# Second attention of a two-layer decoder: values stationary, weights of both heads moving, division ahead of the transposes

## The chip, the cores and the metric

The kernel runs on one core of one Trainium2 chip. The metric is the device time of one execution in microseconds (us); lower is better. The median of 3 runs before the change is 977.81 us (977.59 to 978.05).

## The reference

A decoder trunk of two layers works on one sequence of 256 tokens with 1024 features, in fp32. Each layer is a half-step SwiGLU network, an attention, and a second half-step network, each behind an RMS norm and a modulation computed from a vector `c`. Layer 1 has a differential attention. Layer 2 has the attention that the change touches, a "forgetting" attention with 16 heads of 64 features:

```python
def forgetting_attention(h, w_q, w_o, k, v, F):
    ...
        decay = jnp.transpose(Fqb, (0, 2, 1))[..., None] - F_k[:, :, None, :]
        logits = jnp.einsum('bqhd,bkhd->bhqk', qb, k).astype(jnp.float32) * scale + decay
        logits = jnp.where(causal, logits, -jnp.inf)
        p = jax.nn.softmax(logits, axis=-1)
        return jnp.einsum('bhqk,bkhd->bqhd', p.astype(v.dtype), v)
    ...
    return o.reshape(b, s, B_WIDTH) @ w_o
```

Keys, values and the cumulated forget gates `F` were computed before from the residual stream. With 256 tokens there are two query tiles of 128: tile 0 attends to key block 0, tile 1 to key blocks 0 and 1.

## The kernel before, in words

Activations lie with the features on the partitions and the 256 tokens along the free dimension. All big products run as three fp32r matmuls, since every weight piece is split into a high part `wh` (copied by ScalarE, "ACT") and a low part `wl` (subtracted by VectorE, "DVE"), 1024 columns at a time. The pieces of all layers form one stream (`stream`, L230 to L261) and pass through rings of 6 raw, 6 high and 5 low buffers, so the split runs up to five pieces ahead of their use.

The order of work on each of TensorE ("PE"), ACT and DVE is the order in which the program issues it. The class `InOrder` (L54 to L100) keeps a rough clock for each of these engines at build time. The functions `bg`, `fill_act` and `fill_dve` (L351 to L385) use it to put the splits (`cp_part`, `sub_part`) between other instructions. GpSimd ("POOL") is issued directly; the planner does not know how long its work takes.

`attention_b` (from L1212) handles the 16 heads as 8 pairs `c`. For a pair it needs these steps:

- `load_g`, `decay` (POOL): a DMA that spreads a gate row over the partitions, issued from POOL, and four additions that make `d`, a tile of 384 columns for each head. Its columns are three blocks of 128: query tile 0 with key block 0, then query tile 1 with key blocks 0 and 1.
- `masked` (DVE): the causal mask is added to the two diagonal blocks of `d`, once for each head.
- `scores` (PE): four fp32 matmuls of queries and keys into the first 384 columns of the two banks `sb`, one for each head, with 64 partitions of contraction each.
- `exps`: four times a DVE pass that adds scores and `d` and finds the row extremes, and an ACT exponential with its row sums (`smb`).
- `weights_t` (PE), `weights_out`: six transposes of 128x128 into the banks `wa` and `wb`, copied out by ACT (512 columns, `wta`) and DVE (256 columns, `wtb`).
- `values` (PE): for each head three fp32 matmuls with a transposed weight block as the stationary operand and 64 value columns moving, into the second half of bank `wb`. The result has tokens on the partitions.
- `divide` (DVE): the reciprocal of the row sums and one multiplication of the result (`onb`).
- `out_t` (PE), `out_split`: two transposes into the last 128 columns of the two `sb` banks, so that features come onto the partitions; ACT writes the high part `obh` and DVE the low part `obl`, two instructions each.

These steps are spread over groups: group `t` does the scores and exponentials of pair `t`, the transposes of pair `t-1`, the values and division of pair `t-2`, and the output transposes of pair `t-3`. With 8 pairs there are 11 groups. Before each group stand fills, other PE work given out in small steps (`fills`, L1351): the two last query projections (`lq`) and six of the eight rows of the output projection (`pw`). The numbers of steps are the list in the loop at L1362. `masked(t+1)` and `decay(t+2)` end each group. `OutProj.finish` (L814) then does the last two rows of the output projection, whose inputs are the outputs of pairs 6 and 7, and eight fill steps that were left over.

Of the kernel before, what the change touches and what calls it, by code (L numbers as in the profile page):

```python
# [103 lines left out]
def trunk(ctx, tc, a, out):  # L104
    nc = tc.nc
    InOrder.ready = {}
    pe = InOrder(tc, nc.tensor, 0.0, 1 / 2350)
    act = InOrder(tc, nc.scalar, 0.13, 1 / 1200)
    dve = InOrder(tc, nc.vector, 0.08, 1 / 960)
# [5 lines left out]
    kp = ctx.enter_context(tc.tile_pool(name="kp", bufs=2))  # L115
# [5 lines left out]
    def sbank(name):  # L121
        return pp.tile([P, 512], F32, tag="s", name=name, bufs=2)
# [4 lines left out]
    def bbank(name):  # L127
        return pp.tile([P, 512], F32, tag="tb", name=name)

    mm = pe.matmul  # L130
# [1005 lines left out]
    op, rest = attention_a()  # L1136
# [75 lines left out]
    def attention_b():  # L1212
        ohs = [cp_.tile([P, 512], F32R, tag=f"hidh{j}", name=f"obh{j}") for j in range(4)]
        ols = [cp_.tile([P, 512], F32R, tag=f"hidl{4 + j}", name=f"obl{j}") for j in range(4)]
        o = [(ohs[c // 2][:, (c % 2) * 256:(c % 2) * 256 + 256],
              ols[c // 2][:, (c % 2) * 256:(c % 2) * 256 + 256]) for c in range(NC)]
        q = [cp_.tile([P, 512], F32, tag=f"hidl{j}", name=f"q{j}") for j in range(4)]
        gs, ds, sms = {}, {}, {}

        DT = [f"hidh{4 + j}" for j in range(4)] + ["hidl8", "hidl9"]  # L1220

        def load_g(c):
            g = cp_.tile([P, 512], F32, tag=("hidh10", "hidl10")[c % 2], name=f"fkb{c}")
            nc.gpsimd.dma_start(g, bass.AP(fdram.tensor, fdram.offset + 2 * c * S, [[0, P], [1, 2 * S]]))
            gs[c] = g

        def decay(c):

            for m in range(2):
                hd = 2 * c + m  # L1230
                d = cp_.tile([P, 384], F32, tag=DT[hd % 6], name=f"d{hd}")
                for qt, (c0, w) in enumerate(QT):
                    nc.gpsimd.tensor_scalar(d[:, c0:c0 + w], gs[c][:, m * S:m * S + w],
                                            Fq[:, qt * BH + hd:qt * BH + hd + 1], None, op0=ALU.add)
# [12 lines left out]
        for c in range(2):  # L1247
            load_g(c)
        for c in range(2):
            decay(c)  # L1250
        op = OutProj(o)
        st = {}
        mode[0] = "fill"
        NP = BH // 2

        def scores(c, sb):

            cb = (c % 2) * 256
            for qt, (c0, w) in enumerate(QT):
                for m in range(2):  # L1260
                    rows = slice(m * HD, m * HD + HD)
                    mm(sb[m][:, c0:c0 + w], q[c // 2][rows, cb + qt * P:cb + qt * P + P],
                       kT[c // 2][rows, cb:cb + w], start=True, stop=True)

        def exps(c, sb):
            nm = kp.tile([P, 4], F32, tag="nm", name=f"nmb{c}")
            sm = kp.tile([P, 4], F32, tag="smb", name=f"smb{c}", bufs=3)
            for m in range(2):
                d = ds[2 * c + m]
                for qt, (c0, w) in enumerate(QT):  # L1270
                    cc = 2 * qt + m
                    dve.tensor_tensor_reduce(
                        d[:, c0:c0 + w], sb[m][:, c0:c0 + w], d[:, c0:c0 + w], -0.125, BIG,
                        ALU.add, ALU.min, accum_out=nm[:, cc:cc + 1])
                    act.activation(d[:, c0:c0 + w], d[:, c0:c0 + w], AF.Exp,
                                   bias=nm[:, cc:cc + 1], scale=-1.0, accum_out=sm[:, cc:cc + 1])
            sms[c] = sm

        def weights_t(c, ta, tb):
            for j in range(6):  # L1280
                d, b = ds[2 * c + j // 3], j % 3
                pe.transpose(ta[:, j * P:j * P + P] if j < 4 else tb[:, (j - 4) * P:(j - 3) * P],
                             d[:, b * P:b * P + P], ident)

        def weights_out(c, ta, tb):
            w0 = cp_.tile([P, 512], F32, tag="hidh8", name=f"wta{c}")
            w1 = cp_.tile([P, 256], F32, tag="hidh9", name=f"wtb{c}")
            act.copy(w0, ta)
            dve.tensor_copy(w1, tb[:, :256])
            st[c] = [w0[:, j * P:j * P + P] for j in range(4)] + [w1[:, j * P:j * P + P] for j in range(2)]  # L1290

        def values(c, po):

            for m in range(2):
                hd = 2 * c + m
                wt = st[c][3 * m:3 * m + 3]
                vs = slice((hd % 8) * HD, (hd % 8) * HD + HD)
                v0, v1 = vb[0][hd // 8][:, vs], vb[1][hd // 8][:, vs]
                mm(po[:, m * HD:m * HD + HD], wt[0], v0, start=True, stop=True)
                mm(po[:, P + m * HD:P + m * HD + HD], wt[1], v0, start=True, stop=False)  # L1300
                mm(po[:, P + m * HD:P + m * HD + HD], wt[2], v1, start=False, stop=True)

        def divide(c, po):
            rs = kp.tile([P, 4], F32, tag="rs", name=f"rsb{c}")
            dve.reciprocal(rs, sms[c])
            on = kp.tile([P, 256], F32, tag="w512b", name=f"onb{c}")
            dve.tensor_tensor(on.rearrange("p (g d) -> p g d", g=4), po.rearrange("p (g d) -> p g d", g=4),
                              rs.rearrange("p (g o) -> p g o", o=1).to_broadcast([P, 4, HD]), op=ALU.mult)
            st[c] = on

        def out_t(c, pz):
            for qt in range(2):
                pe.transpose(pz[qt], st[c][:, qt * P:qt * P + P], ident)

        def out_split(c, pz):
            oh, ol = o[c]
            for qt in range(2):
                act.copy(oh[:, qt * P:qt * P + P], pz[qt])
            for qt in range(2):
                qs = slice(qt * P, qt * P + P)  # L1320
                dve.tensor_tensor(ol[:, qs], pz[qt], oh[:, qs].bitcast(F32), op=ALU.subtract)

        def group(t):

            cs, cw, cv, co = (c if 0 <= c < NP else None for c in (t, t - 1, t - 2, t - 3))
            sb = [sbank(f"sb{t}_{m}") for m in range(2)] if cs is not None or co is not None else None
            ta = abank(f"wa{t}") if cw is not None else None
            tb = bbank(f"wb{t}") if cw is not None or cv is not None else None
            if co is not None:
                pz = [sb[m][:, 384:] for m in range(2)]  # L1330
                out_t(co, pz)
            if cs is not None:
                scores(cs, sb)
            if cv is not None:
                values(cv, tb[:, 256:])
            if cw is not None:
                weights_t(cw, ta, tb)
            if co is not None:
                out_split(co, pz)
            if cs is not None:  # L1340
                exps(cs, sb)
            if cv is not None:
                divide(cv, tb[:, 256:])
            if cw is not None:
                weights_out(cw, ta, tb)
            if t + 1 < NP:
                masked(t + 1)
            if t + 2 < NP:
                decay(t + 2)

        def fills():  # L1351
            for j in (2, 3):
                for _ in late_pair("wq", q[j], r, f"lq{j}"):
                    yield
                    yield
            for _ in range(6):
                for _ in op.steps():
                    yield

        masked(0)  # L1360
        fill = fills()
        for t, n in enumerate((3, 9, 7, 7, 7, 7, 7, 7, 7, 6, 5)):  # L1362
            for _ in range(n):
                next(fill)
            group(t)
        return op, fill
# [135 lines left out]
```

## Time and profile before

| what | value |
|---|---|
| median of 3 runs | 977.81 us |
| the profiled execution, its own time | 978.77 us |
| its span, first to last instruction | 976.9 us |
| PE busy | 965.2 us (99%) |
| DVE busy | 815.0 us (83%) |
| ACT busy | 551.1 us (56%) |
| POOL busy | 82.0 us (8%) |
| granted TensorE clock | 0.998 |
| the second attention in the span | from about 717 to 789 us |

The profile is that of one execution. A group row gives the line, the engine, the operation, the tiles written and read (out<-in), the shapes and the count, then the busy time, the mean of one in ns, and the idle time of that engine just before, with what ended it. Nearly all rows have line L99, the place in `InOrder` where every instruction is issued, so tiles tell them apart. An fp32 matmul appears as two instructions, a transpose and an fp32r matmul as one. A row of a timeline gives start, length, engine, tiles and count; neighbouring instructions of one kind are merged in it, under the shape of the first. A row with engine shares gives a stretch of time and, for each engine in turn (PE, weight loads, DVE, ACT, POOL), how long it was busy in it. The ends of matmuls are modelled; starts are measured.

### The profile page before, as it was taken

The numbers are of one execution on the slowest core, as the hardware profiler recorded it, in microseconds if no ns is written. First come the engines' busy times: TensorE is split into PE (matmuls) and PEld (weight loads), VectorE is DVE, ScalarE is ACT, GpSimd is POOL, SyncE is SP. The second block draws the span as 40 slices with busy tenths as digits, with TensorE's granted clock in tenths as the row PEclk, the third lists the DMA queues.
The fourth block names the chain that finished last, engine by engine and source line by source line (L and its number), as shares of the span: only waits on it lengthen the run. The fifth ranks groups of instructions, "written<-read, shape, count | busy, mean of one in ns | idle before, by whom it ended". The sixth has DMA issues, their size and how long they took to land.

```text
span 976.9 us, 20500 instructions
## 1 busy us (share of the span) xinstructions
PE 965.2 (99%) x8130; PEld 940.8 (96%) x8130; DVE 815.0 (83%) x1370; ACT 551.1 (56%) x901; POOL 82.0 (8%) x117
## 2 busy tenths in 40 slices
PE   8999999999999999999999999999999999999997
PEld 6999999998999999999998999999999999999997
DVE  6989979889999999878898989989977699555565
ACT  5366545566777645455576554445567576455441
POOL 0000200000112000000000000000048124300000
PEclk9999999999999999999999999999999999999999
DMA  9998899967876699788959899988875237977651
GB/s 358 414 352 265 336 369 337 353 223 269 299 240 233 203 379 371 296 290 309 330 183 361 306 336 341 354 303 314 302 259 163 88 108 231 265 155 267 186 150 44
DMA packets 69057, 267.16 MB, mean 273 GB/s; under 512 B 9273, under 2 KB 10065, under 8 KB 58850
## 3 DMA queue, kind: packets, MB, share of 16 engines
q1 hardware_dynamic: 66016, 259.69, 75.8%
q0 software_dynamic: 2656, 5.86, 2.0%
q8 instruction: 63, 1.03, 0.5%
q10 hardware_dynamic: 290, 0.32, 0.1%
q14 instruction: 32, 0.26, 0.1%
HBM read 263.70 MB, written 2.65 MB: 273 GB/s over the span
## 4 chain that ended last, share of the span: by engine, by line
PE 97%; DVE 1%; DMA 1%; ACT 0%; issue 0%; SPq 0%; DVEq 0%
PE po L99 25%; PE pg L99 21%; PE pu L99 21%; PE pf L99 5%; PE pv L99 5%; PE pw L99 4%; PE lp L99 4%; PE pqk L99 3%; PE wb L99 1%; PE lq L99 1%; PE lu L99 1%; PE lg L99 1%; PE pk L99 1%; PE sb L99 1%; DMA ada<-in_ada 1%; PE s L99 1%
## 5 line engine op out<-in xcount | busy, mean ns | idle before, releaser
L99 ACT CAST wh<-raw 128x1024 fp32r<-128x1024 f32 (+1 forms) x360 | 347.0, 974 | 208.9 <-PE pu L99 87.7
L99 DVE TENSOR_TENSOR wl<-raw,wh 128x1024 fp32r<-128x1024 f32 (+1 forms) x360 | 399.1, 1128 | 74.3 <-ACT sg L99 20.7
L99 DVE CUSTOM_DVE_ANT_0 ada<-ada,cact,vecs 128x1024 f32<-128x1024 f32 x160 | 203.6, 1279 | 0.5 <-DMA ada<-in_ada 0.5
L99 PE MATMUL pg<-HH,wh 128*128 128x256 f32 x608 | 168.0, 276 | 0.0
L99 PE MATMUL pg<-HH,wl 128*128 128x256 f32 x608 | 167.9, 276 | 0.0
L99 PE MATMUL pu<-HH,wh 128*128 128x256 f32 x608 | 167.9, 276 | 0.0
L99 PE MATMUL pg<-HL,wh 128*128 128x256 f32 x608 | 167.9, 276 | 0.0
L99 PE MATMUL pu<-HL,wh 128*128 128x256 f32 x608 | 167.9, 276 | 0.0
L99 PE MATMUL pu<-HH,wl 128*128 128x256 f32 x608 | 167.9, 276 | 0.0
L99 PE MATMUL po<-hidh,wh 128*128 128x256 f32 x528 | 145.7, 276 | 0.0
L99 PE MATMUL po<-hidh,wl 128*128 128x256 f32 x528 | 145.7, 276 | 0.0
L99 PE MATMUL po<-hidl,wh 128*128 128x256 f32 x528 | 145.7, 276 | 0.0
L99 PEld LDWEIGHTS pg<-HH,wh 128*128 128x128 f32 x608 | 114.1, 188 | 0.7 <-ACT hidh L99 0.6
L99 PEld LDWEIGHTS pg<-HH,wl 128*128 128x128 f32 x608 | 114.2, 188 | 0.0
L99 PEld LDWEIGHTS pu<-HH,wh 128*128 128x128 f32 x608 | 114.2, 188 | 0.0
L99 PEld LDWEIGHTS pg<-HL,wh 128*128 128x128 f32 x608 | 114.2, 188 | 0.0
L99 PEld LDWEIGHTS pu<-HH,wl 128*128 128x128 f32 x608 | 114.1, 188 | 0.0
L99 PEld LDWEIGHTS pu<-HL,wh 128*128 128x128 f32 x608 | 114.1, 188 | 0.0
L99 PEld LDWEIGHTS po<-hidh,wh 128*128 128x128 f32 x528 | 99.1, 188 | 0.0
L99 PEld LDWEIGHTS po<-hidh,wl 128*128 128x128 f32 x528 | 99.1, 188 | 0.0
L99 PEld LDWEIGHTS po<-hidl,wh 128*128 128x128 f32 x528 | 99.1, 188 | 0.0
L99 ACT CAST hidh<-hf 128x512 fp32r<-128x512 f32 x44 | 27.3, 621 | 40.6 <-DVE hf L99 40.6
(227 smaller groups left out, 1872.5 us busy)
## 6 DMA issues: line engine op xcount, KB each, us to landing
raw<-in_win SPq DMA_DIRECT2D x176, 512.0 KB, 6.6
ada<-in_ada SPq DMA_DIRECT2D x79, 1024.0 KB, 7.1
raw<-in_wout SPq DMA_DIRECT2D x48, 384.0 KB, 5.5
raw<-in_wout SPq DMA_DIRECT2D x48, 320.0 KB, 5.1
raw<-in_wqk SPq DMA_DIRECT2D x16, 512.0 KB, 5.6
raw<-in_wo SPq DMA_DIRECT2D x16, 512.0 KB, 5.0
raw<-in_wlast SPq DMA_DIRECT2D x16, 512.0 KB, 4.3
raw<-in_wv SPq DMA_DIRECT2D x8, 512.0 KB, 7.5
```

Source lines behind the costliest of these rows:

```text
L99: return self.tc.keep_in_program_order(f(*args, **kw))
```

## The change

Steps of the attention are computed in another layout. The stationary operand of the value product becomes the 128 value columns of both heads of the pair, and the transposed weights of both heads move: one fp32 matmul of 512 columns for key block 0 (both query tiles, both heads) and one of 256 columns for key block 1. The result `po` has 128 output features on the partitions (64 of each head) and, for each head, 256 tokens along the free dimension; each head's own half is read and the other half is not used. The output transposes are thereby gone, and the high and low parts are taken from `po` directly, 64 partitions by 256 columns each.

The division by the row sums moves ahead of the weight transposes: the reciprocal (`inverse`, DVE) is issued in the group of the exponentials, and `divide` multiplies `d` itself, the first 128 columns of each head on POOL, the other 256 on ACT. The six weight transposes go to bank `wa` (four) and to the last 128 columns of the two `sb` banks of the current group (two), where the output transposes went before. A group handles pairs `t`, `t-1` and `t-2`, so there are ten groups; the same 72 fill steps are given out in a new list.

```diff
-        def weights_out(c, ta, tb):
+        def inverse(c):
+            rs = kp.tile([P, 4], F32, tag="rs", name=f"rsb{c}")
+            dve.reciprocal(rs, sms[c])
+            sms[c] = rs
+
+        def divide(c):
+
+            rs = sms[c]
+            for m in range(2):
+                d = ds[2 * c + m]
+                nc.gpsimd.tensor_scalar(d[:, :P], d[:, :P], rs[:, m:m + 1], None, op0=ALU.mult)
+                act.activation(d[:, P:], d[:, P:], AF.Copy, scale=rs[:, 2 + m:3 + m])
+
+        def weights_t(c, ta, sb):
+
+            for m in range(2):
+                d = ds[2 * c + m]
+                for b in range(2):
+                    pe.transpose(ta[:, m * S + b * P:m * S + b * P + P], d[:, b * P:b * P + P], ident)
+            for m in range(2):
+                pe.transpose(sb[m][:, 384:], ds[2 * c + m][:, 2 * P:3 * P], ident)
+
+        def weights_out(c, ta, sb):
             w0 = cp_.tile([P, 512], F32, tag="hidh8", name=f"wta{c}")
             w1 = cp_.tile([P, 256], F32, tag="hidh9", name=f"wtb{c}")
             act.copy(w0, ta)
-            dve.tensor_copy(w1, tb[:, :256])
+            for m in range(2):
+                dve.tensor_copy(w1[:, m * P:m * P + P], sb[m][:, 384:])
+            st[c] = w0, w1
...
         def values(c, po):
 
+            w0, w1 = st[c]
+            vs = slice((c % 4) * P, (c % 4) * P + P)
+            mm(po, vb[0][c // 4][:, vs], w0, start=True, stop=False, skip_group_check=True)
+            mm(po.rearrange("p (m t) -> p m t", m=2)[:, :, P:], vb[1][c // 4][:, vs],
+               w1.rearrange("p (m t) -> p m t", m=2), start=False, stop=True, skip_group_check=True)
+
+        def halves(c, po):
+            oh, ol = o[c]
             for m in range(2):
...
+                rows = slice(m * HD, m * HD + HD)
+                yield oh[rows], ol[rows], po[rows, m * S:m * S + S]
 
         def group(t):
...
             if cs is not None:
                 scores(cs, sb)
             if cv is not None:
-                values(cv, tb[:, 256:])
-            if cw is not None:
-                weights_t(cw, ta, tb)
-            if co is not None:
-                out_split(co, pz)
+                values(cv, po)
             if cs is not None:
                 exps(cs, sb)
+            if cw is not None:
+                weights_t(cw, ta, sb)
             if cv is not None:
-                divide(cv, tb[:, 256:])
+                for oh, ol, p in halves(cv, po):
+                    act.copy(oh, p)
             if cw is not None:
-                weights_out(cw, ta, tb)
+                weights_out(cw, ta, sb)
+            if cs is not None:
+                inverse(cs)
+            if cv is not None:
+                for oh, ol, p in halves(cv, po):
+                    dve.tensor_tensor(ol, p, oh.bitcast(F32), op=ALU.subtract)
+            if cs is not None:
+                divide(cs)
             if t + 1 < NP:
                 masked(t + 1)
             if t + 2 < NP:
...
-        for t, n in enumerate((3, 9, 7, 7, 7, 7, 7, 7, 7, 6, 5)):
+        for t, n in enumerate((3, 9, 7, 7, 7, 7, 8, 8, 8, 8)):
```

More of the change, by code (lines that the diff above doesn't have):

```diff
@@ L1277, in exps @@
             sms[c] = sm
[L1279 to L1283, printed above, removed]
-        def weights_out(c, ta, tb):
+        def inverse(c):
[16 more added lines that the diff above has]
+        def weights_out(c, ta, sb):
             w0 = cp_.tile([P, 512], F32, tag="hidh8", name=f"wta{c}")
@@ L1288, in weights_out @@
             act.copy(w0, ta)
-            dve.tensor_copy(w1, tb[:, :256])
-            st[c] = [w0[:, j * P:j * P + P] for j in range(4)] + [w1[:, j * P:j * P + P] for j in range(2)]
+            for m in range(2):
+                dve.tensor_copy(w1[:, m * P:m * P + P], sb[m][:, 384:])
+            st[c] = w0, w1
         def values(c, po):
-            for m in range(2):
[L1295 to L1321, printed above, removed]
+            w0, w1 = st[c]
+            vs = slice((c % 4) * P, (c % 4) * P + P)
+            mm(po, vb[0][c // 4][:, vs], w0, start=True, stop=False, skip_group_check=True)
@@ L1323, in group @@
+            mm(po.rearrange("p (m t) -> p m t", m=2)[:, :, P:], vb[1][c // 4][:, vs],
+               w1.rearrange("p (m t) -> p m t", m=2), start=False, stop=True, skip_group_check=True)
+        def halves(c, po):
+            oh, ol = o[c]
+            for m in range(2):
+                rows = slice(m * HD, m * HD + HD)
+                yield oh[rows], ol[rows], po[rows, m * S:m * S + S]
         def group(t):
-            cs, cw, cv, co = (c if 0 <= c < NP else None for c in (t, t - 1, t - 2, t - 3))
@@ L1326, in group @@
-            sb = [sbank(f"sb{t}_{m}") for m in range(2)] if cs is not None or co is not None else None
+            cs, cw, cv = (c if 0 <= c < NP else None for c in (t, t - 1, t - 2))
+            sb = [sbank(f"sb{t}_{m}") for m in range(2)] if cs is not None or cw is not None else None
             ta = abank(f"wa{t}") if cw is not None else None
-            tb = bbank(f"wb{t}") if cw is not None or cv is not None else None
-            if co is not None:
-                pz = [sb[m][:, 384:] for m in range(2)]
-                out_t(co, pz)
+            po = bbank(f"po{t}") if cv is not None else None
@@ L1334, in group @@
             if cv is not None:
-                values(cv, tb[:, 256:])
-            if cw is not None:
-                weights_t(cw, ta, tb)
-            if co is not None:
-                out_split(co, pz)
+                values(cv, po)
             if cs is not None:
                 exps(cs, sb)
+            if cw is not None:
+                weights_t(cw, ta, sb)
             if cv is not None:
-                divide(cv, tb[:, 256:])
+                for oh, ol, p in halves(cv, po):
+                    act.copy(oh, p)
             if cw is not None:
-                weights_out(cw, ta, tb)
+                weights_out(cw, ta, sb)
[6 more added lines that the diff above has]
+                divide(cs)
             if t + 1 < NP:
```

## The prediction

> **What bounds the kernel now.** I read the page first, for what ended last, and then the chain that ended last in order of time between 700 and 800 us, where the second attention lies. The page:
>
> ```profile
> PE 97%; DVE 1%; DMA 1%; ACT 0%; issue 0%; SPq 0%; DVEq 0%
> ```
>
> TensorE (PE) is the chain from end to end, so the time changes by what PE's own work loses or gains and by every new wait of PE. The chain in order of time gives the prices (start, length, tile, instructions):
>
> ```profile
> 719.85 0.43 PE psn L99 x2
> ...
> 730.42 0.86 PE sb L99 x8
> ...
> 739.79 1.48 PE wb L99 x12
> 741.28 0.45 PE wa L99 x4
> 741.72 0.22 PE wb L99 x2
> ...
> 753.09 2.40 PE pw L99 x21
> 755.49 1.07 PE sb L99 x10
> ...
> 772.80 1.29 PE wb L99 x12
> ```
>
> Read one group of the attention here. `sb` is the scores of a pair of heads: 0.86 us for 8 instructions (each fp32 matmul is two), and 1.07 for 10 where the two output transposes come first, so those two cost 0.21. `wb` x12 is the six value matmuls of 64 columns: 1.48 behind scores, 1.29 where no scores precede (at 772.80). `wa` x4 and `wb` x2 are the six weight transposes, 0.11 each. `pw` x21 is fill work from the output projection, 0.114 each. In that stretch no piece of the chain belongs to another engine: today the attention never stops PE.
>
> How waits fall must be read before the change. This is VectorE (DVE) alone:
>
> ```profile
> 738.69 1.33 DVE L99 TENSOR_TENSOR wl<-raw,wh 128x1024 fp32r<-128x1024 f32 x1
> ...
> 741.05 0.16 DVE L99 RECIPROCAL rsb<-smb 128x4 f32<-128x4 f32 x1
> 741.98 0.42 DVE L99 TENSOR_TENSOR onb<-wb,rsb 128x256 f32<-128x256 f32 x1 [0.76 <-PE wb L99]
> ```
>
> The value result and the last two weight transposes lie in different halves of one PSUM bank. The division `onb` reads only the half that the values had finished at 741.28, yet it sat idle until the transposes into the other half ended at 741.94. So in this program a reader of a bank stands behind every earlier writer of that bank, whichever columns it reads. I take it that a writer likewise stands behind earlier readers.
>
> **What the change does to PE's own work.** Removed: two output transposes in each of 8 groups, 8 x 0.21 = 1.7 us. Values: twelve instructions of 64 columns become four, two of 512 columns and two of 256. The `psn` row is one fp32 matmul of 256 columns, two instructions in 0.43, so 512 + 256 columns are 0.86 + 0.43 = 1.29. That is what the old twelve take where no scores precede. Behind scores they take 0.19 more; the new ones follow the scores too, so I expect that surcharge to stay. Bounds for the values: nothing, or 0.19 saved in each of the six groups with scores and values, 1.1 us. I take nothing. The eleventh group, which goes, held only the transposes counted above, and the fills are 72 in both versions. PE's gain is 1.7 us, with 2.8 as the other end.
>
> [...]
>
> **The first new wait: the banks of the scores.** The last two weight transposes now go into the free last quarters of the two banks that hold this group's scores, so they stand behind DVE's pass over those scores. From group 2 on PE has 1.48 of values and 0.45 of transposes between the scores and these two. Group 1 has no values. DVE, ACT and PE around it:
>
> ```profile
> 732.66 0.79 DVE L99 TENSOR_TENSOR d<-d,tri 128x256 f32<-128x256 f32 x2
> 733.37 1.22 DVE L99 TENSOR_TENSOR wl<-raw,wh 128x1024 fp32r<-128x1024 f32 x1
> 735.26 0.29 DVE L99 CUSTOM_DVE_ANT_0 d<-sb,d 128x128 f32<-128x128 f32 x1 [0.67 <-PE sb L99]
> ...
> 736.04 0.42 DVE L99 CUSTOM_DVE_ANT_0 d<-sb,d 128x256 f32<-128x256 f32 x1
> ```
> ```profile
> 733.55 0.19 ACT L99 ACTIVATION_READ_ACCUMULATOR d<-d,nmb 128x1 f32 x1
> ```
> ```profile
> 734.31 0.93 PE L99 MATMUL sb<-kT,q 64*128 64x128 f32 x8
> 735.16 0.66 PE L99 MATMUL wa<-tri,d 128*128 128x128 f32 x4
> ```
>
> DVE's pass takes 1.2 us, 735.26 to 736.46, so from group 2 on it is covered if DVE starts it promptly. In group 1 PE would reach the fifth transpose at 735.16 + 0.45 = 735.6; that alone is a wait of 0.85. But the change also puts the reciprocal ahead of DVE's mask addition (`d<-d,tri`), and it must wait for the last sum of group 0's exponentials, at 733.74. Behind it queue the mask, 0.79, and the split of a weight piece (`wl`), 1.22: 733.74 + 0.16 + 0.79 + 1.22 = 735.9 instead of 734.6. DVE's pass of group 1 then runs from 735.9 to 737.1, and the wait becomes 1.5. Bounds 0.85 and 1.5 (0 if writers do not stand behind readers, which the `onb` row speaks against); I take 1.5, because the split comes before that pass today and I see nothing that moves it.
>
> **The second new wait: GpSimd.** Half of each division now runs on GpSimd (POOL), two instructions of 128x128, between the decays of four instructions each and the DMA issue for a later decay. Its queue now, and the price of one instruction (least, median, most; then the mean):
>
> ```profile
> 733.92 3.52 POOL L1233 TENSOR_SCALAR d<-fkb,Fq 128x128 f32<-128x128 f32 x4
> 737.74 0.58 POOL L1224 DMA_DIRECT2D fkb<-fdram  x1 [0.30 <-PE lq L99]
> 738.37 3.92 POOL L1233 TENSOR_SCALAR d<-fkb,Fq 128x128 f32<-128x128 f32 x4
> ...
> 743.21 3.77 POOL L1233 TENSOR_SCALAR d<-fkb,Fq 128x128 f32<-128x128 f32 x4
> ...
> 747.90 4.19 POOL L1233 TENSOR_SCALAR d<-fkb,Fq 128x128 f32<-128x128 f32 x4
> ...
> 753.01 3.04 POOL L1233 TENSOR_SCALAR d<-fkb,Fq 128x128 f32<-128x128 f32 x4
> 758.54 4.08 POOL L1233 TENSOR_SCALAR d<-fkb,Fq 128x128 f32<-128x128 f32 x4 [2.48 <-PE wa L99]
> ```
> ```profile
> L1233 POOL TENSOR_SCALAR d<-fkb,Fq x32: 592/916/2072, 722.8 to 761.7; 128x128 f32<-128x128 f32 x16, 128x256 f32<-128x256 f32 x16
> ```
> ```profile
> L1233 POOL TENSOR_SCALAR d<-fkb,Fq 128x128 f32<-128x128 f32 x16 | 13.4, 835 | 7.3 <-DMA fkb<-fdram 4.6 <-PE wa L99 2.5
> ```
>
> From 733.92 to 756.05 POOL has no pause but those of 0.30 around its DMA issues; only the last decay waited for PE. The lead that it has built up is all that the change can spend. A 128x128 instruction takes 0.59 at least and 0.835 on average, so a division is 1.2 to 1.7 us; I take 1.2 and let the disturbance stand in the decays. The disturbance has a cause that the rows show: the decay at 753.01 takes 3.04, the one at 738.37, with the `wl` of 738.69 at its side, 3.92, so 0.88 was lost beside a `wl` of 1.33. [...]
>
> Now the chain on POOL. The first division can start at 733.9, when the reciprocal is done, with the mask and the `wl` from above beside it; its end is between 735.2 and 736.7, and I take 736.2. Four rounds follow up to the division that group 5 needs: decays 2 to 5 as they stand, 3.52 + 3.92 + 3.77 + 4.19 = 15.4; four DMA issues with their pauses, 0.93 each (738.37 less the end at 733.92 + 3.52), 3.7; four divisions, 4.8. End: 736.2 + 23.9 = 760.1. PE, without this wait, begins group 5 at 755.49 - 0.42 (groups 3 and 4 without output transposes) + 1.5 = 756.6 and wants the second head's weights after 0.86 + 1.48 + 0.22, at 759.1. So PE waits 1.0 us in all, spread over groups 2 to 5; from decay 6 on there is no DMA issue and from group 6 on no new decay, and POOL catches up. Lower bound: decays at 3.04 give 756.9 and no wait. Upper bound: divisions at 1.67 and the later start give 762.5, a wait of 3.4. I keep 1.0, as its decays are measured ones.
>
> **What is hidden.** ACT gains two scaled copies of 256 columns, and its output copies grow from two of 128x128 to two of 64x256. DVE gets two copies of 128 columns for one of 256 and wider subtractions, and loses the old division of 0.42: about even. The stretch with the most POOL work, and the nearest ACT row:
>
> ```profile
> 752.00:756.00 4.00, 4.00 (x39) 3.83 (x40) 2.52 (x11) 2.58 (x10) 3.66 (x6) 1.00 0.60 197
> ```
> ```profile
> L99 ACT ACTIVATE q<-lt,lcol 128x256 f32<-128x256 f32 x6 | 2.7, 501 | 0.7 <-DVE lt L99 0.4
> ```
>
> Of 4 us DVE is busy for 2.52, ACT for 2.58, POOL for 3.66. Two ACT copies at 0.50 and about 0.2 for the wider output copies are 1.2 in a group of some 5.6 us, against 2.0 free: covered, and if the cover were gone, at most 1.2 per group late at the next transposes. DVE's mask now waits for the later decay, with weight splits queued behind it; they are made ahead of their use, and I cost their delay at nothing. At the end the last outputs come straight from the values: two ACT copies, overlapping to some 0.8, and 0.4 of DVE before the third matmul that needs them, behind eight others, 8 x 0.114 = 0.9. Bounds 0 and 0.6; I take 0.2.
>
> **The sum.** -1.7 + 1.5 + 1.0 + 0.2 = +1.0 us. The profiled execution took 978.77 (its span and 1.9 around it), 0.96 above the median of 977.81; it becomes 979.8, and the median 978.8.
>
> **Rivals.** (B) The waits are covered: POOL's lead suffices, and of group 1's wait 0.85 or less remains. For it: POOL itself waited 2.48 for PE at 758.54. Against: it had no pause before. -1.7 + 0.85 = -0.9, 976.9; without any wait 976.1. (C) POOL bounds groups 1 to 5, because a `wl` in each round stops it for its whole 1.22: four rounds at undisturbed decays are 4 x (3.04 + 0.93 + 1.2 + 1.22) = 25.6 and end at 761.8, and with the upper bound above at 762.5. The wait is 2.7 to 3.4, the sum +2.7 to +3.4, 980.5 to 981.2: slower. It decides once a round on POOL exceeds 6.2 us, against PE's 5.6 or so per group. For it: 3.66 busy of 4.00. Against: only 0.88 of 1.33 was lost. [...] (D) The values gain more than I allow: 0.19 in each of eight groups, 1.5, with waits as in B: -1.7 - 1.5 + 0.85 = -2.4, 975.4. Against: the `psn` row. [...] That the change does not do what it says I exclude, since its instructions are written out.
>
> **How the numbers follow.** Chances: forecast 0.48, B 0.19, C 0.25, D 0.08. 0.2% is 1.96 us, about what a measurement of this kernel can tell from no change: faster is below 975.9, slower above 979.8. The forecast's own range is 977.5 to 980.5, with a quarter of its chance above 979.8. Faster: D, 0.08. Slower: C and that quarter, 0.25 + 0.13 = 0.38, rounded. Same: the rest, 0.54. The range from 976.1 (B without waits) to 981.6 (just beyond C) leaves out D and what follows if waits cascade.
>
> **What would show it.** In the profile after: no transposes of `onb`; the values, four instructions per group, in 1.29 us or up to 1.5 behind the scores; among PE's waits one for the transposes into `sb`, ended by DVE's pass, longest in group 1 at about 1.5; another for `wa` or `sb` ended by POOL, 1 to 2 us together in groups 2 to 5 and none after; POOL without a pause until some 765; DVE's mask waiting for POOL by a us or two. Wrong would be: no wait of PE on DVE in group 1 (then writers do not stand behind readers), values well under 1.29, or PE waiting for ACT.

## The result, and the profile after

| | median of the runs | lowest to highest | the profiled execution, its span |
|---|---|---|---|
| before | 978.05 us (7 runs) | 977.59 to 982.83 | 978.77, 976.9 |
| after | 986.20 us (7 runs) | 984.99 to 986.61 | 985.36, 983.5 |

The changed kernel takes 1.0065 times as long (ratio of the means, 95% interval 1.0046 to 1.0084), which is 6.4 us; the medians lie 8.15 apart, since two of the seven runs before took 982.27 and 982.83. The forecast was 978.8, with a range of 976.1 to 981.6. It was wrong.

Nearly all of it lies in the second attention. A clean measure is the stretch from the first scores (`sb`, group 0) to the first `lg` matmul behind the output projection, both starts taken from PE's timeline. It takes 58.37 us before (730.36 to 788.72) and 65.49 after (729.69 to 795.18), 7.1 more. The rest of the kernel differs by half a microsecond.

The page of after has the engines' busy times, and the chain that ended last:

```profile
PE 966.9 (98%) x8050; PEld 936.9 (95%) x8050; DVE 816.3 (83%) x1370; ACT 560.6 (57%) x917; POOL 91.6 (9%) x133
...
PE 88%; issue 6%; POOL 2%; DVE 2%; ACT 1%; DMA 1%; POOLq 0%
```

Before, the chain was 97% PE and held nothing of POOL. Now 2% of the span, some 20 us, are POOL's. These shares tell which engines the chain runs through, and not how much was lost: nearly all of the 6% of "issue" is one piece of 57.05 us, ahead of POOL's DMA of a gate row at 716.48, in which PE went on with other work. The waits of PE in the whole kernel (us in total, times, longest) say for what:

```profile
PE wa L99 <- POOL d L1289: 4.9, 2, 4.6
...
PE pw L99 <- DVE obl L99: 0.4, 1, 0.4
```

Line L1289 is the division. The forecast had put 1.0 us on this wait, over several groups, and here one piece of it is 4.6. This is PE around that place, and at two others that the forecast spoke of:

```profile
733.65 0.93 PE L99 MATMUL sb<-kT,q 64*128 64x128 f32 x8
739.22 1.26 PE L99 MATMUL wa<-tri,d 128*128 128x128 f32 x4 [4.64 <-POOL d L1289]
740.26 0.64 PE L99 MATMUL sb<-tri,d 128*128 128x128 f32 x2
...
745.55 1.12 PE L99 MATMUL po<-wta,vb 128*128 128x512 f32 x2
746.52 0.59 PE L99 MATMUL po<-wtb,vb 128*128 128x256 f32 x2
...
786.92 0.39 PE L99 MATMUL pw<-obh,wh 128*128 128x256 f32 x1
787.14 0.28 PE L99 MATMUL pw<-obh,wl 128*128 128x256 f32 x1
787.81 0.39 PE L99 MATMUL pw<-obl,wh 128*128 128x256 f32 x1 [0.39 <-DVE obl L99]
```

In group 1 the scores start at 733.65 and take 0.86. The first weight transpose starts at 739.22, so PE stands still for some 4.7 us. The values (745.55 to 746.95, where the next tile starts) take 1.39, as they did before. At the end the first matmuls of the last pair wait twice, for the high part `obh` (786.92 follows a start at 786.50) and for the low part `obl`.

Why the division came so late is in POOL's own timeline (start, length, line, tiles, count, idle time before and what ended it):

```profile
733.34 4.27 POOL L1233 TENSOR_SCALAR d<-fkb,Fq 128x128 f32<-128x128 f32 x4
737.91 0.58 POOL L1224 DMA_DIRECT2D fkb<-fdram  x1 [0.30 <-POOL d L1233]
738.54 1.19 POOL L1289 TENSOR_SCALAR d<-d,rsb 128x128 f32<-128x128 f32 x2
740.95 3.23 POOL L1233 TENSOR_SCALAR d<-fkb,Fq 128x128 f32<-128x128 f32 x4 [1.22 <-PE sb L99]
744.47 0.59 POOL L1224 DMA_DIRECT2D fkb<-fdram  x1 [0.30 <-POOL d L1233]
745.10 1.19 POOL L1289 TENSOR_SCALAR d<-d,rsb 128x128 f32<-128x128 f32 x2
747.91 3.23 POOL L1233 TENSOR_SCALAR d<-fkb,Fq 128x128 f32<-128x128 f32 x4 [1.62 <-ACT d L99]
751.12 1.18 POOL L1289 TENSOR_SCALAR d<-d,rsb 128x128 f32<-128x128 f32 x2
```

The program issues the division of pair 0 ahead of the decay of pair 2. On the chip it stands behind that decay (733.34) and, here, its DMA issue. The divisions of pairs 1 to 5 stand behind the decay of the pair two further on in the same way; for pairs 6 and 7 there is none. PE, ACT and DVE keep the order in which the program issues, because `InOrder` asks for it; nothing asks for it on POOL, and there the framework's scheduler chose an order of its own. Before, only decays and their DMA issues stood in this stretch of POOL's queue, and their order could not go wrong. The reciprocal that the first division needs is done at 733.37 on DVE (733.19 and 0.18 long), when the decay of pair 2 has just begun. The division starts at 738.54.

The row at 740.95 shows the second half of the trouble. The decay waited there 1.22 us for PE. The `d` tiles rotate through six buffers, three pairs, so the decay of pair 3 writes the buffers of pair 0, which PE must have transposed first. The late order thus closes a loop: division of pair `t` on POOL, its transposes on PE, the decay of pair `t+3` on POOL, the division of pair `t+1` behind it. From the first to the second division the loop takes 745.10 - 738.54 = 6.6 us, where a group of PE took 5.7 before (scores at 755.64 and 761.34). The chain that ended last shows the same further on:

```profile
760.02 3.63 POOL d L1233 x3
763.66 1.17 POOL d L1289 x2
764.83 0.04 issue
764.88 0.44 PE wa L99 x2
```

Decay, division, transposes: PE waits at the end of it.

One more thing happens in group 1. A view by stretches of 4 us shows PE's busy time first and the granted clock behind POOL's:

```profile
736.00:740.00 4.00, 0.65 (x3) 0.42 (x4) 0.46 (x4) 1.45 (x7) 3.39 (x6) 0.95 0.59 171
740.00:744.00 4.00, 4.00 (x23) 4.00 (x23) 2.11 (x7) 2.29 (x6) 3.05 (x4) 0.62 0.13 33
```

After the idle time the granted clock fell to a mean of 0.62, and the 24 fills behind it took 4.15 us from start to start, against 3.07 before.

From PE's starts the 7.1 us divide like this: the wait in group 1 +5.4 (scores and six transposes together 6.90 against 1.49), the slow fills behind it +1.1, later waits for divisions in groups 3 to 6 +1.9, the end +0.8 (72 matmuls in 9.45 against 8.66), the output transposes -2.1 and the last values -0.2. That sums to +6.9; the rest is spread over the fills.

### The profile page after: what moved, and what is told of

Read it like the earlier page. It is cut to its first block, busy times and chain, and to the rows that moved or that the text cites. A ratio compares the mean times of both kernels' runs of the same rounds, so it can differ in the third digit from the quotient of the medians.

```text
span 983.5 us, 20390 instructions
## 1 busy us (share of the span) xinstructions
PE 966.9 (98%) x8050; PEld 936.9 (95%) x8050; DVE 816.3 (83%) x1370; ACT 560.6 (57%) x917; POOL 91.6 (9%) x133
## 4 chain that ended last, share of the span: by engine, by line
PE 88%; issue 6%; POOL 2%; DVE 2%; ACT 1%; DMA 1%; POOLq 0%
PE pg L99 21%; PE pu L99 21%; PE po L99 20%; PE pf L99 5%; PE pv L99 5%; PE pw L99 4%; PE pqk L99 3%; PE lp L99 2%; POOL d L1233 2%; PE lu L99 1%; PE lg L99 1%; PE pk L99 1%; PE s L99 1%; PE lq L99 1%; DMA fkb<-fdram 1%
```

## The experiments

All kernels are variations of the changed one. Kernels that stand below one "before" ran on the same chip as its runs. The stretch is that from the first scores to the first `lg`, from the profiled execution; the ratio is that of the means, against the kernel before.

| kernel | median, us | ratio, 95% interval | stretch, us |
|---|---|---|---|
| before | 978.16 | | 58.37 |
| 1: POOL in program order | 979.14 | 1.0005, 0.9996 to 1.0014 | 58.91 |
| 2: ACT divides all | 982.14 | 1.0039, 1.0026 to 1.0052 | 61.71 |
| 3: POOL's part left out | 979.67 | 1.0013, 1.0002 to 1.0024 | 59.25 |
| 4: as 2, other bank in group 1 | 981.81 | 1.0035, 1.0021 to 1.0049 | 62.14 |
| before | 978.21 | | |
| 5: as 1, other bank in group 1 | 978.31 | 1.0001, 0.9992 to 1.0009 | 58.60 |
| 6: as 1, two fills behind the last group | 978.16 | 1.0004, 0.9993 to 1.0016 | 58.13 |
| 7: 5 and 6 together | 978.03 | 1.0004, 0.9995 to 1.0012 | 57.89 |
| 8: as 6, last two transposes later | 981.97 | 1.0044, 1.0031 to 1.0057 | 62.02 |
| before | 978.18 | | |
| 9: as 7, ACT divides the first pair | 976.82 | 0.9986, 0.9975 to 0.9997 | 56.89 |
| 10: late order, PE kept busy | 987.29 | 1.0103, 1.0088 to 1.0118 | 66.45 |
| 11: late order written out | 988.08 | 1.0114, 1.0089 to 1.0139 | 66.67 |

In the cuts of code, `keep` is `tc.keep_in_program_order`, the call by which `InOrder` asks for the program's order; "..." stands for what is left out.

My theory was that the order of POOL's queue makes the loss, and that the terms of the forecast hold once that order is as the program has it. The rivals were that POOL has too much work in any order, and that PE's wait belongs to the banks of the scores.

**1. POOL in program order.**

```
-   nc.gpsimd.dma_start(g, ...)
+   keep(nc.gpsimd.dma_start(g, ...))
...
-   nc.gpsimd.tensor_scalar(d[:, c0:c0 + w], ...)
+   keep(nc.gpsimd.tensor_scalar(d[:, c0:c0 + w], ...))
...
-   nc.gpsimd.tensor_scalar(d[:, :P], d[:, :P], rs[:, m:m + 1], ...)
+   keep(nc.gpsimd.tensor_scalar(d[:, :P], d[:, :P], rs[:, m:m + 1], ...))
```

> Only the order of GpSimd's queue is changed: decay, DMA issue and division of the second attention run in the order in which the program writes them, so each division stands ahead of the next decay. Theory (order): the long wait of TensorE in group 1 comes from decay 2 standing ahead of division 0; with the order of the program that wait falls from 5.0 us to 1 to 2 us, TensorE's clock stays at full speed after it, and the kernel lands 1 to 2 us above the kernel before, about 5 us under the changed kernel. Rival (throughput): GpSimd has too much work in groups 1 to 5 whatever the order; the wait is only spread over groups 2 to 6, and the time stays within 1.5 us of the changed kernel.

979.14 us. The order alone takes 6.6 us of the stretch away (65.49 to 58.91), and the rival of too much work falls. POOL's timeline of this kernel, then PE's, then DVE's:

```profile
734.21 2.24 POOL L1290 TENSOR_SCALAR d<-d,rsb 128x128 f32<-128x128 f32 x2 [0.18 <-DVE rsb L99]
736.43 2.99 POOL L1234 TENSOR_SCALAR d<-fkb,Fq 128x128 f32<-128x128 f32 x4
739.72 0.59 POOL L1225 DMA_DIRECT2D fkb<-fdram  x1 [0.30 <-POOL d L1234]
740.35 1.20 POOL L1290 TENSOR_SCALAR d<-d,rsb 128x128 f32<-128x128 f32 x2
```
```profile
735.31 0.44 PE L99 MATMUL wa<-tri,d 128*128 128x128 f32 x2
736.50 0.44 PE L99 MATMUL wa<-tri,d 128*128 128x128 f32 x2 [0.75 <-POOL d L1290]
736.77 0.69 PE L99 MATMUL sb<-tri,d 128*128 128x128 f32 x2
```
```profile
734.01 0.73 DVE L99 TENSOR_TENSOR d<-d,tri 128x256 f32<-128x256 f32 x2
734.66 1.31 DVE L99 TENSOR_TENSOR wl<-raw,wh 128x1024 fp32r<-128x1024 f32 x1
```

The first division now starts at 734.21 and ends at 736.45, where the forecast had 733.9 and 736.2. But PE wants the second head's weights of pair 0 already in group 1, at about 735.5, and waits for them. The division took 2.24 beside the mask and the split on DVE, and 1.20 a round later.

**2. ACT divides everything**, so POOL has its old work alone.

```
-   nc.gpsimd.tensor_scalar(d[:, :P], d[:, :P], rs[:, m:m + 1], None, op0=ALU.mult)
+   act.activation(d[:, :P], d[:, :P], AF.Copy, scale=rs[:, m:m + 1])
```

> The division of the first 128 columns of each head moves from GpSimd to ScalarE, which then divides all 384 columns; GpSimd does what it did before the change. Theory (order) and rival (throughput) both expect every wait of TensorE for GpSimd to go, and 0 to 2 us above the kernel before: 1.7 us less work of TensorE against the wait behind the banks of the scores in group 1 (1 to 1.5), and the wait at the end (0.8). A second rival (ScalarE becomes the bound) expects new waits for ScalarE and more than 3 us above the kernel before.

982.14, some 4 us above the kernel before, where theory and first rival had at most 2. The second rival had the size, over 3, but not the place: no wait on POOL is left, and PE waits for DVE's pass over the scores and not for ACT. PE in groups 1 and 5, DVE and ACT ahead of group 5:

```profile
735.92 0.33 PE L99 MATMUL sb<-tri,d 128*128 128x128 f32 x1 [0.68 <-DVE nmb L99]
...
759.46 0.33 PE L99 MATMUL sb<-tri,d 128*128 128x128 f32 x1 [0.82 <-DVE nmb L99]
```
```profile
757.51 1.23 DVE L99 TENSOR_TENSOR wl<-raw,wh 128x1024 fp32r<-128x1024 f32 x1 [1.28 <-ACT wh L99]
```
```profile
755.05 1.49 ACT L99 ACTIVATE d<-d,rsb 128x128 f32<-128x128 f32 x4
756.45 1.98 ACT L99 CAST wh<-raw 128x1024 fp32r<-128x1024 f32 x2
```

Four divisions on ACT (1.49) push its cast of a weight piece to 756.45, DVE's split of that piece stands at the head of DVE's queue waiting for the cast, and DVE's pass over the scores stands behind the split. So ACT's work comes out as a wait of PE on DVE, two engines further. Free time on ACT was not the question, but who stands behind it in a fixed order.

**3. POOL's part left out.** The first 128 columns of `d` are not divided at all; everything else stays.

```
-   nc.gpsimd.tensor_scalar(d[:, :P], d[:, :P], rs[:, m:m + 1], None, op0=ALU.mult)
```

> The division of the first 128 columns of each head, GpSimd's part, is left out altogether, so the weights of the first 128 queries stay undivided; ScalarE still divides its 256 columns. Theory and rival both expect the time of the version with ScalarE alone or up to 1 us less: this is the price of GpSimd's part without any cover elsewhere. If it stays 3 us or more above the kernel before, GpSimd is not the cause.

979.67. Theory and rival had it within 1 us of kernel 2; it is 2.5 less, since ACT's two extra divisions in each group are gone as well. So with no division on POOL at all, the kernel is not faster than with one in the right order. In group 1 the six transposes take 1.38 and 0.64, some 1.4 us of wait, now all of it for DVE's pass; group 4 and the end give 0.8 each.

**4. The other bank in group 1**, on top of kernel 2. Group 1 has no values, so the last two transposes can go into their bank.

```
-   pe.transpose(sb[m][:, 384:], ds[2 * c + m][:, 2 * P:3 * P], ident)
+   pe.transpose(wb[m], ds[2 * c + m][:, 2 * P:3 * P], ident)
...
+   wb = [po[:, m * P:m * P + P] if t == 1 else sb[m][:, 384:] for m in range(2)]
```

> As the version with ScalarE alone, and in group 1 only the last two weight transposes go to the free bank of the value result instead of the banks of the scores. Theory of the bank wait (a writer stands behind every earlier reader of its bank): 0.8 to 1.5 us under the version with ScalarE alone, and no wait of TensorE for VectorE's pass in group 1. Rival (writers do not stand behind readers): the same time within 0.3 us, as no such wait exists, or group 1 waits for the division itself.

The wait in group 1 goes: six transposes in 0.67 us in place of 2.02, which is 1.34 less. In this program a writer does stand behind earlier readers of its bank, as the forecast took it. But the total, which was to fall by 0.8 to 1.5, did not move, 981.81. For one thing a wait came back in group 4, whose six transposes take 2.67 in place of 0.58; in kernel 2 the second long wait was in group 5, with 2.06:

```profile
734.73 0.38 PE L99 MATMUL po<-tri,d 128*128 128x128 f32 x2
...
753.13 0.33 PE L99 MATMUL sb<-tri,d 128*128 128x128 f32 x1 [1.43 <-DVE nmb L99]
753.69 0.33 PE L99 MATMUL sb<-tri,d 128*128 128x128 f32 x1 [0.23 <-DVE nmb L99]
```
```profile
748.00:752.00 4.00, 3.71 (x24) 2.42 (x22) 2.95 (x9) 3.57 (x11) 2.05 (x3) 1.00 0.22 64
752.00:756.00 4.00, 2.64 (x14) 2.45 (x15) 3.04 (x12) 3.24 (x13) 2.37 (x4) 0.78 0.52 153
756.00:760.00 4.00, 4.00 (x23) 3.04 (x22) 1.97 (x10) 1.99 (x7) 0.63 (x1) 0.79 0.03 8
```

For another, the granted clock fell here too, to 0.78 and 0.79 in two stretches, and 21 fills took 4.17 us against 2.57 (in kernel 1 from 754.36 to 756.93). Over the whole attention the transposes take 0.5 us less than in kernel 2 and the fills 1.0 more, so in the profiled execution the lower clock, and not the returned wait alone, kept the time from falling.

**5. The other bank in group 1, with POOL in program order**: the edits of 1 and 4.

> GpSimd in program order as in the first experiment (979.14), and the last two weight transposes of group 1 alone go into the bank of the values' result, which is free there. My theory: what is left of the loss in that kernel is the wait of group 1 behind VectorE's pass (transposes 1.46 + 0.45 against 0.44 + 0.14 elsewhere, 1.33 us), 0.5 of the same kind in group 4, and 0.8 at the end. So 1.3 less: 977.8, with group 1's six transposes in about 0.6 and the two other waits where they were. The rival: PE arrives 1.3 us earlier at groups 2 to 5, where GpSimd or VectorE are then late; the wait moves there (waits of PE on GpSimd of over 0.8, or a bank wait in groups 3 to 5 of over 0.6), and the time stays at 978.5 to 979.1.

The stretch is 0.31 shorter, not 1.3; the theory missed the size. Four transposes into `wa` still take 1.46, and only the 0.45 of the last two becomes 0.14. In kernel 1 the wait for the bank was nearly hidden behind the wait for the first division: two causes for one pause, of which the later one pays.

**6. Two fills behind the last group**, with POOL in program order.

```
-   for t, n in enumerate((3, 9, 7, 7, 7, 7, 8, 8, 8, 8)):
+   for t, n in enumerate((3, 9, 7, 7, 7, 7, 8, 8, 8, 6)):
        ...
+   for _ in range(2):
+       next(fill)
```

> GpSimd in program order, and two of the eight fills ahead of the last group stand behind it instead, so that 18 matmuls in place of 12... that is, 6 more matmuls (0.7 us) lie between the last values and the first matmul that needs their split. My theory: the 0.8 at the end (72 matmuls of the output projection's last part in 9.46 against 8.66) is the wait for the last copies and subtractions. It goes, the 72 matmuls behind the two fills take 8.7 again: 978.3. The rival: the 0.8 is not that wait (the accumulators, or the norm's column work behind them); then the time stays at 979.1, with gaps in the same places.

As expected: 78 matmuls at the end take 9.45 where 72 took 9.46, and the stretch is 0.8 shorter. The 0.8 at the end was the wait for the last pair's outputs, and six matmuls cover it.

**7. Both.**

> Both edits on top of GpSimd's program order. My theory adds them: 979.14 - 1.3 - 0.8 = 977.0, which is about 1 us under the kernel before, as 1.7 to 2.1 us of output transposes are gone and only the 0.5 of group 4 and small waits are left. The rival: waits move rather than go, 978 to 979.

The edits add, 58.91 - 0.31 - 0.79 = 57.81 against 57.89 measured, but as the fifth gave less, the time is 978.03, no different from before. What is left in group 1 is the first division.

**8. The last two transposes two fills later**, in all groups, on top of kernel 6; their copies to SBUF go with them.

```
            for k in range(n):
                next(fill)
+               if k == 1 and later:
+                   next(later.pop(), None)
```

> GpSimd in program order, the end as in the sixth kernel, and in every group the last two transposes and their copies stand behind the first two fills of the next group (0.7 us of other PE work), in the scores' banks as in the change. My theory: no group waits for VectorE's pass by more than 0.6 (group 1: 1.33 less 0.7), so 979.14 - 0.8 - 0.7 - 0.5 = 977.1, a little less if the copies do not matter. The rival: the copies now queue on VectorE behind the mask, which waits for GpSimd's decay, and behind a split of a weight piece; then the second value matmul waits for VectorE by 0.3 or more in several groups, and the time is 978 to 980.

981.97: the rival, at another place than it said, and above its 978 to 980. PE waits 2.9 us in four places for the copies `wtb`, though not at the values but at the next scores, which want the same banks. PE's row in group 3, and DVE's queue ahead of it:

```profile
748.68 1.12 PE L99 MATMUL sb<-kT,q 64*128 64x128 f32 x8 [0.98 <-DVE wtb L99]
```
```profile
745.54 1.20 DVE L99 TENSOR_TENSOR wl<-raw,wh 128x1024 fp32r<-128x1024 f32 x1
746.66 0.85 DVE L99 TENSOR_TENSOR obl<-po,obh 64x256 fp32r<-64x256 f32 x2
747.54 0.76 DVE L99 TENSOR_TENSOR d<-d,tri 128x256 f32<-128x256 f32 x2
748.33 0.49 DVE L99 COPY wtb<-sb 128x128 f32<-128x128 f32 x2
```

Moving the transposes also moved their copies behind a split, a subtraction and the mask.

**9. ACT divides the first pair alone**, on top of kernel 7.

```
+   if c:
        keep(nc.gpsimd.tensor_scalar(d[:, :P], d[:, :P], rs[:, m:m + 1], None, op0=ALU.mult))
+   else:
+       act.activation(d[:, :P], d[:, :P], AF.Copy, scale=rs[:, m:m + 1])
```

> The seventh kernel (GpSimd in program order, group 1's last transposes in the other bank, two fills behind the last group), with the division of the first pair alone done wholly on ScalarE. My theory now: what was left in group 1 of the seventh kernel (four transposes in 1.47 us against 0.44 elsewhere) is not VectorE's pass but the first division on GpSimd, which took 2.24 us beside a mask and a weight split of VectorE instead of 1.19, and ended 0.8 us after PE wanted it. On ScalarE that wait goes: 978.03 - 0.9 = 977.1, group 1's four transposes in 0.44 to 0.55. The rival: ScalarE's two copies more (0.8 us) delay the casts of a weight piece, and with them VectorE's pass of a later group, as where ScalarE divides in all groups; then a bank wait of 0.5 to 1.5 turns up in groups 2 to 4 and the time stays at 978.0 or above.

976.82, a ratio of 0.9986 (0.9975 to 0.9997): faster than the kernel before by 1.4 us, and than the changed one by 9 if the medians of the two sets of runs are put side by side. Group 1 has no wait left:

```profile
733.27 0.93 PE L99 MATMUL sb<-kT,q 64*128 64x128 f32 x8
734.12 0.70 PE L99 MATMUL wa<-tri,d 128*128 128x128 f32 x4
734.66 0.38 PE L99 MATMUL po<-tri,d 128*128 128x128 f32 x2
```

**11. The late order written out**: kernel 1, but the program itself issues each pair's division behind the decay and its DMA. Told ahead of 10, which builds on it.

```
            if t + 2 < NP:
                decay(t + 2)
+           if cs is not None:
+               divide_pool(cs)
```

> The changed kernel with GpSimd's instructions in program order, as in the first experiment, but the program now puts each pair's division behind the decay two pairs on and its DMA issue, which is the order that GpSimd had in the changed kernel's trace. My theory: the order alone makes the loss, so this gives the changed kernel's time again, 985 to 986.5, with PE idle for 4.5 to 5 us in group 1. The rival: not the order but something else in asking for it changed the time (where the divisions stand against ScalarE's and VectorE's work); then 979 to 981.

988.08: the loss is back, and a little more, as here all DMA issues stand ahead of the divisions, where the scheduler had put some behind. Kernels 1 and 11 differ in nothing but the order of POOL's queue, so that this order makes the loss is shown from both sides.

**10. PE kept busy while it waits**: kernel 11 with 40 transposes of a constant, their result not used, ahead of group 1's weight transposes.

```
+   if t == 1:
+       idle = bbank("idle")
+       for _ in range(40):
+           pe.transpose(idle[:, :P], ident, ident)
```

> The kernel with GpSimd's late order written out, and 40 transposes of a constant (0.11 us each, 4.4 in all, result not used) ahead of group 1's weight transposes, so that PE works while it waits. My theory: of the loss in group 1 about 1.1 us is not the wait but what follows it, a granted clock of 0.62 for some 2.5 us after 5 us of idling. With PE busy the clock stays at 1.00, group 1's 24 fills behind it take 3.1 us again instead of 4.15, and the time is 1.0 to 1.1 below the kernel with the same order, the wait for GpSimd being as late as it was. The rival: the fills are slow for another reason (their operands, or the other engines late behind the wait); they take about 4.1 again and the time is the same or higher.

The stretch behind the wait, in kernel 11 and then in kernel 10:

```profile
740.00:744.00 4.00, 4.00 (x23) 4.00 (x24) 2.07 (x7) 2.19 (x6) 2.95 (x4) 0.64 0.11 36
```
```profile
740.00:744.00 4.00, 4.00 (x36) 3.81 (x36) 3.10 (x8) 3.12 (x8) 3.25 (x4) 1.00 0.09 33
```

The clock stays at 1.00, and group 1's 24 fills take 3.07 in place of 4.04. In this the theory holds. But the time it promised did not come: the stretch is 66.45 against 66.67, and the intervals of the two ratios overlap. POOL sets the pace. Its divisions start at 738.64, 745.20, 752.06 and 758.98 in kernel 11 and at 738.69, 745.72, 752.66 and 758.85 in kernel 10. PE, a microsecond early, waits for the next division instead.

## Why the prediction was wrong, point by point

**The step that failed** is the sentence "The first division can start at 733.9, when the reciprocal is done", and with it the chain of "Four rounds" on POOL. It took POOL to work in the order of the source. The division started at 738.54, and from there the loop through the `d` buffers, which the forecast did not have, set the pace up to group 6. The forecast had said itself that the lead POOL had built up was all that the change could spend; with the division behind a decay, the whole lead lies ahead of the division and is worth nothing to it. Rival C, "POOL bounds groups 1 to 5", comes nearest in kind, but its mechanism (DVE's splits stopping POOL) and its 980.5 to 981.2 were not what happened.

**A second error in the same step** showed only in kernel 1. The forecast compared POOL with PE in group 5 and left out group 1, where PE wants the first division at about 735.5 and the forecast's own end for it was 736.2. That the forecast's sum and kernel 1 agree (978.8, 979.14) is therefore partly luck: POOL's wait of 1.0 came in group 1 and hid most of the bank's, while the bank's wait of 0.5 in group 4 and 0.6 more at the end were not in the sum, and 0.6 more than forecast came off for the output transposes and the last values.

**The bank of the scores** was right for this program (kernel 4: 1.34 against the 1.5 of the forecast), and right in time: DVE's pass ran from 735.89 to 737.07 in kernel 1, forecast 735.9 to 737.1. In the changed kernel it cost nothing, because PE came to these banks only at 740.26, when the pass was long done. So the forecast's own sign against it, no wait of PE on DVE in group 1, came true for another reason than the one it named.

**PE's own work.** The values were taken as equal, 1.29 and 0.19 more behind scores. By starts they are 1.39 behind scores and 1.29 without, in both kernels; only those of the last pair are shorter, 1.10 against 1.26. The values have 96 weight loads before (`wb<-vb`) and 32 after (`po`), and the measured change in their time is under 0.2 us. (A quarter of 0.48 is 0.12 and not 0.13; the forecast's time does not rest on it.) The output transposes were put at 1.7 and are 2.1 by starts: five groups at 0.31, three at 0.22, 0.22 and 0.14. I had used the chain's lengths, 1.07 less 0.86, and a start-to-start time holds the small gap behind them too.

**The division's price on POOL**, 1.2 us, is right where nothing disturbs it (1.18 to 1.20). For the first one the forecast had taken 2.3 (733.9 to 736.2), and in kernel 1 it is 2.24, so 1.05 were lost beside a mask of 0.73 and a split of 1.31. Later divisions there were to be 1.67 at most; one of them took 2.26 (from 750.52), also beside a split (from 750.93, 1.39 long). That these delays make the loss is not so: in kernel 1 the same neighbours stand beside POOL, and its stretch is 0.5 us longer than before, not 7.

**ACT as hidden work** was right as far as the changed kernel goes: up to the last group PE never waited for it. But it has less room than the forecast's 0.8 us per group: two more divisions of 128 columns per group cost 2.5 us of the stretch (kernel 2 against kernel 3, which does without them).

**The end** was put at 0.2 and measured 0.8. Both the high and the low part came late (786.92, 787.81), and kernel 6 shows that six matmuls of cover are what was missing.

What stays open is why the clock fell in kernel 4, after a pause of 1.43 us, and by what rule the scheduler put the decay first.

## What to carry to other kernels

Before you cost a queue in the order of the source, check that something holds this engine to that order; here three engines were held to it and the fourth was not, and one reordered step cost more than the whole change could bring. Follow each new step from its producer to its first consumer in every stage, the first one above all, since the stage with the least other work has the least cover. And when a wait is removed, ask for the next one behind it: in kernels 4 and 10 a pause that was taken away was paid again at another place, in kernel 5 the same pause had a second cause, and only with all causes of group 1's pause and the wait at the end gone (kernel 9) was the change worth its 1.4 us.

## What the hardware showed beside this

PE's idle time of 4.7 us in the changed kernel was followed by a mean granted clock of 0.62 from 740 to 744, and with PE busy in the same place (kernel 10) it stayed at 1.00. In kernel 4 the longest pause there was 1.43 us, with another of 0.23 behind it, and the clock fell to 0.78, so a shorter pause was also followed by a lower clock, and it cost 1.6 us of fills; the pauses of 0.7 to 0.8 in kernels 1 and 2 left it at 1.00. The length of a pause alone did not decide it: near the start of the kernel before, PE stood still for 2.46 us (up to 14.95), and the granted clock was 1.00 from 10.8 to 18.0.

Finer stretches of the changed kernel show that the clock did not fall by degrees there: it is 1.00 from 739.4 to 739.6, 0.50 to 0.51 in every piece from 739.6 to 743.0, 0.96 from 743.0 to 743.2 and 1.00 behind. So it stood at half for some 3.4 us. For kernels 11 and 4 I estimate the same 3.4 us from the means of two neighbouring stretches of 4 us, if the clock was either full or half: 0.93 and 0.64 from 736 to 744 in kernel 11, 0.78 and 0.79 from 752 to 760 in kernel 4. That holds after the pause of 1.43 as after those of 4.6. PE had already started again when the clock fell: at 739.22 in the changed kernel, and at 753.69 in kernel 4, whose fills start 0.12 apart up to 754.21 and 0.22 apart from 754.36.
